# The up projection in products of 256 columns: two feature tiles to a PSUM bank, relu and its square on ScalarE

## The chip, the cores and the metric

The kernel runs on one core of a Trainium2 chip. Its matrix engine is TensorE (PE in the profile, with its weight loads shown apart as PEld), its elementwise engines are VectorE (DVE) and ScalarE (ACT); SyncE (SP) issues most DMAs, and GpSimd (POOL) does little here. Matrix products are written to PSUM, in banks of 2 KB per partition (512 float32 columns); everything else lies in SBUF. The metric is the time of one execution in microseconds of device time. Before the change it is 1237.76 us, the median of three runs (1237.73 to 1237.81).

## What is computed

One layer of a decoder trunk on 256 tokens of width 2048, in float32. A combined input projection feeds a pooling branch and a convolution branch; gated, they are mixed, projected and added to the residual stream. Then comes the part that the change touches, the feed-forward block, with a hidden width of 8192:

```python
h = h + rms_norm(m @ w_o[l], g_post_mix[l])
u = rms_norm(h, g_pre_mlp[l])
f = jnp.square(jax.nn.relu(u @ w_up[l])) @ w_down[l]
h = h + rms_norm(f, g_post_mlp[l])
```

## The kernel before

**Split products.** Every float32 operand `x` of a matrix product is kept as two parts of a faster matrix type: `hi`, the rounded value, and `lo`, what rounding left over. A product is then the sum of three: hi·hi, hi·lo and lo·hi. For the weights ScalarE writes `hi` (L178) and VectorE subtracts to get `lo` (L181), chunk by chunk: a chunk is 512 rows by 512 columns of a weight matrix, 1 MB, loaded by one DMA from SyncE. `fetch()` (L198) opens the chunk two ahead of the one in use, splits it, and then runs the functions that wait in the list `late`. There are three buffers each for the raw chunk, for `hi` and for `lo`.

**The feed-forward block** runs in four passes `i` over the hidden width (loop at L994). Each pass computes 2048 hidden features for all 256 tokens and then adds their share of the down projection. The up projection of a pass is four blocks `h` of 512 features; a block is one call of `project` (L362), which goes through four chunks of 512 input rows. In a block the weights are the stationary operand, so that the result has features on the partitions and the 256 tokens along the columns. A feature tile is 128 features wide, so a block has four of them, `j`, each with a PSUM bank of its own. For each tile and each of the 16 groups of 128 input rows there are two products, issued by `mm2` (L353): one of 512 columns with `hi` of the weights (L344), whose moving operand holds the hi part of the tokens in its first 256 columns and the lo part in the other 256, and one of 256 columns with `lo` of the weights and the hi part of the tokens (L350). So the two halves of the bank must be added at the end. The first block of the first pass, `up00`, is written out apart (from L892) and is not changed.

**Evacuation of a tile** (L841): ScalarE copies the first half of the bank to SBUF (`halves`, L381), VectorE adds the second half (L383), VectorE multiplies the sum with its maximum with zero, which is relu squared (L844), and later, from the list `late`, ScalarE writes the hi part to `f_act` (L388) and VectorE the lo part (L389). `f_act` is the stationary operand of the down projection.

**The down projection** `project_t` (L600) keeps the tokens' hidden features as the stationary operand and streams the weights, 512 columns to a product (`block_t`, L590). Its last block is written out at the end of the kernel; for the second half of the tokens its 512 columns are cut in two halves of 256 (`last_half`, L1007), so that there the same three products are 256 columns wide, with the stationary operands hi, hi and lo in turn.

**Order.** The kernel sets the order of each engine's instructions by hand: they run on each engine as the program issues them, and engines wait for each other by semaphores. `drain` hands out small pieces of other work (in the first pass, the squares of the residual stream, L786) between the products of a chunk; `flush(1)` runs all but the newest of the `late` functions ahead of an evacuation. The pool `psA` has six banks for accumulators.

Of the kernel before, what the change touches and what calls it, by code (L numbers as in the profile page):

```python
# [8 lines left out]
F32 = mybir.dt.float32  # L9
F32R = mybir.dt.float32r  # L10
AF = mybir.ActivationFunctionType
# [3 lines left out]
P = 128  # L15
CK = 4
CW = 512
# [5 lines left out]
def hybrid_block(ctx: ExitStack, tc: tile.TileContext, ins: dict, out: bass.AP):  # L23
    nc = tc.nc
    x = ins["x"][0]
    meta = ins["meta"]
    T, D = x.shape
# [3 lines left out]
    KD = D // P  # L31
# [18 lines left out]
    big = ctx.enter_context(tc.tile_pool(name="big", bufs=1))  # L50
# [6 lines left out]
    def f32(ap):  # L57
        return ap.bitcast(F32)

    def acc_tile(name):  # L60
        return psA.tile([P, CW], F32, tag="acc", name=name)
# [9 lines left out]
    late = []  # L71
# [5 lines left out]
    def flush(n=0):  # L77
        while len(late) > n:
            late.pop(0)()

    def drain(us=None):

        credit["us"] += us or 0.0
        while pending and (us is None or credit["us"] >= pending[0][0]):
            cost, f = pending[0]
            if f is late and late:
                if us is not None:
                    break
                flush()
            pending.pop(0)  # L90
            if callable(f):
                f()
                if us is not None:
                    credit["us"] -= cost
            elif f is None and us is not None:
                break
        credit["us"] = min(credit["us"], pending[0][0]) if pending else 0.0
# [61 lines left out]
    def open_chunk():  # L159
        n = at["n"]  # L160
        at["n"] += 1
        src, (rows, width) = stream[n]
        raw = raws.tile([P, CK * CW], F32, tag="raw", name=f"raw_{n}")
        if n in spare:
            both = big.tile([P, 2, CK * CW], F32R, tag=spare[n], name=f"parts_{n}")
            hi, lo = both[:, 0, :], both[:, 1, :]
        else:
            hi, lo = part_tile("hi", n), part_tile("lo", n)
        raw, hi, lo = (t.rearrange("p (k c) -> p k c", k=rows) for t in (raw, hi, lo))
        pieces = rows if n < FIRST + 1 else 1  # L170
        k = rows // pieces
        loads = 4 if n < FIRST else 1
        for i in range(loads):
            sl = slice(i * rows // loads, (i + 1) * rows // loads)
            nc.sync.dma_start(raw[:, sl, :], src[:, sl, :])

        def high(sl):
            nc.scalar.copy(hi[:, sl, :], raw[:, sl, :])  # L178

        def low(sl):  # L180
            nc.vector.tensor_sub(lo[:, sl, :], raw[:, sl, :], f32(hi[:, sl, :]))  # L181

        def piece(i):
            def f():
                sl = slice(i * k, (i + 1) * k)
                high(sl)
                low(sl)
            return f
        todo = [piece(i) for i in range(pieces)]
        if n in spare:  # L190
            todo = [lambda: high(slice(0, rows)), lambda: low(slice(0, rows))]
        opened.append((hi, lo, todo))

    def split_pieces(c):
        while opened[c][2]:
            opened[c][2].pop(0)()

    def fetch(ahead=2):  # L198

        for c in range(ahead + 1):  # L200
            if c == len(opened) and at["n"] < len(stream):
                open_chunk()
            if c < len(opened):
                split_pieces(c)
        flush()
        return opened.pop(0)[:2]
# [146 lines left out]
    def mm2(acc, hi, lo, act, k, cs, first, last):  # L353


        mm2_high(acc, hi, act, k, cs, first, stop=last)
        mm2_low(acc, lo, act, k, cs, stop=last)

    def acc_tiles(name, n=CW // P):
        return [acc_tile(f"acc_{name}_{j}") for j in range(n)]  # L360

    def project(act, nk, evac, name, mm=mm2, width=CW, shape=HALF, fill=0.0):  # L362

        ck, cw = shape
        accs = [acc[:, :width] for acc in acc_tiles(name, cw // P)]
        for kc in range(nk // ck):
            hi, lo = fetch()
            for j, acc in enumerate(accs):
                for k in range(ck):
                    kk = kc * ck + k  # L370
                    mm(acc, hi, lo, act, (k, kk), slice(j * P, (j + 1) * P), kk == 0, kk == nk - 1)
                if kc == nk // ck - 1:
                    flush(1)
                    evac(j, acc)
                if fill:
                    drain(fill * P / cw)

    def halves(acc, name):

        t = tmp.tile([P, T], F32, tag="v", bufs=5, name=f"half_{name}")  # L380
        nc.scalar.copy(t, acc[:, :T])  # L381
        s = tmp.tile([P, T], F32, tag="v", bufs=5, name=f"sum_{name}")
        nc.vector.tensor_add(s, t, acc[:, T:])  # L383
        return s

    def split(dst, k, src):
        def f():
            nc.scalar.copy(dst[:, k, 0, :], src)  # L388
            nc.vector.tensor_sub(dst[:, k, 1, :], src, f32(dst[:, k, 0, :]))  # L389
        late.append(f)  # L390
# [209 lines left out]
    def project_t(act, nk, evac, name, fill=0.0):  # L600
        accs = acc_tiles(name, NT)
        for kc in range(nk // CK):
            hi, lo = fetch()
            for t, acc in enumerate(accs):
                block_t(acc, hi, lo, act, kc, nk, t)
                if kc == nk // CK - 1:
                    evac(t, acc)
                if fill:
                    drain(fill / NT)
            while after:  # L610
                after.pop(0)()
# [37 lines left out]
    hi, lo = fetch()  # L649
    for g in range(NG):  # L650
        for j in range(GK):
            q = g * GK + j
            acc = acc_tile(f"acc_grp_{q}")[:, :T]
# [158 lines left out]
    u2 = m  # L812
# [23 lines left out]
    f_act = []  # L836
# [4 lines left out]
    def evac_up(j0):  # L841
        def f(j, acc):
            s = halves(acc, f"up_{j0 + j}")
            nc.vector.scalar_tensor_tensor(s, s, 0.0, s, op0=ALU.max, op1=ALU.mult)  # L844
            split(f_act[(j0 + j) // (KD // 2)], (j0 + j) % (KD // 2), s)
        return f

    assert NT == 2 and NB == 4 and CK == 4  # L850
# [85 lines left out]
    hi, lo = fetch()  # L936
# [3 lines left out]
    for j, acc in enumerate(accs):  # L940
        for k in range(CK):
            kk = 3 * CK + k
            mm2(acc, hi, lo, u2, (k, kk), slice(j * P, (j + 1) * P), False, kk == KD - 1)
        flush(1)
        evac_up(0)(j, acc)
    ssq2 = const.tile([P, NT, NB], F32, name="ssq2")


# [18 lines left out]
    def evac_down(i, n):  # L967
        sl = block(n)

        def f(t, acc):  # L970
            if i == 0:
                nc.vector.tensor_copy(F[:, t, sl], acc)
                return
            nc.vector.tensor_add(F[:, t, sl], F[:, t, sl], acc)
            if i == NP - 1:
                square_of(F[:, t, sl], norm3.ssq, t, n, scale=r2[:, t:t + 1])
                times_g(t, sl)
                if n == NB - 2:
                    norm3.start(t)
        return f  # L980
# [12 lines left out]

    for i in range(NP):  # L994
        for h in range(1 if i == 0 else 0, NB):
            project(u2, KD, evac_up(h * CW // P), f"up{i}{h}", shape=(CK, CW), fill=1.0)
        for n in range(NB):
            if i < NP - 1 or n < NB - 1:
                project_t(f_of, KD, evac_down(i, n), f"dn{i}{n}")
# [11 lines left out]
    n = KD // CK - 3  # L1011
    for kc in range(n):
        hi, lo = fetch()
# [12 lines left out]
    for h, cs in enumerate(col_halves):  # L1026
# [3 lines left out]
        s = tmp.tile([P, HALF_CW], F32, tag="v", bufs=5, name=f"last_{h}")  # L1030
# [37 lines left out]
```

## Time and profile before

| | |
|---|---|
| time, median of 3 runs | 1237.76 us |
| the profiled execution's own time | 1238.2 us |
| its span, first to last instruction | 1236.3 us |
| instructions in the profile | 15686 |
| bytes moved by DMA | 237.22 MB |

The profile is one execution. Its page gives each engine's busy time and, for groups of equal instructions, the count, the busy time in all, the mean of one in ns and what ended the idle time before them. A product's entry in a timeline has its start, its duration and its tile of PSUM; products overlap in the pipeline, so what one of them costs is read from the distance between starts and not from its duration. The rows that matter are quoted in the prediction.

### The profile page before, as it was taken

The numbers are of one execution on the slowest core, as the hardware profiler recorded it, in microseconds if no ns is written. First come the engines' busy times: TensorE is split into PE (matmuls) and PEld (weight loads), VectorE is DVE, ScalarE is ACT, GpSimd is POOL, SyncE is SP. The second block draws the span as 40 slices with busy tenths as digits, with TensorE's granted clock in tenths as the row PEclk, the third lists the DMA queues.
The fourth block names the chain that finished last, engine by engine and source line by source line (L and its number), as shares of the span: only waits on it lengthen the run. The fifth ranks groups of instructions, "written<-read, shape, count | busy, mean of one in ns | idle before, by whom it ended". The sixth has DMA issues, their size and how long they took to land.

```text
span 1236.3 us, 15686 instructions
## 1 busy us (share of the span) xinstructions
PE 1224.7 (99%) x6572; PEld 1061.3 (86%) x6572; DVE 807.6 (65%) x938; ACT 541.9 (44%) x571; POOL 6.2 (0%) x18
## 2 busy tenths in 40 slices
PE   9999999999999999999999999999999999999997
PEld 7999988888888888898888888888888888888886
DVE  5799988999676654585654556654475544556555
ACT  6533334444584433555433345433344433435432
POOL 1000000000000000000000000000000000000000
PEclk9999999999999999999999999999999999999999
DMA  8655556556548656646556566556566556566551
GB/s 260 207 181 179 171 171 204 188 188 204 175 165 298 212 205 204 204 142 200 175 200 197 183 199 200 180 199 200 185 194 204 182 193 204 176 201 203 187 187 68
DMA packets 130757, 237.22 MB, mean 192 GB/s; under 512 B 3985, under 2 KB 29905, under 8 KB 130160
## 3 DMA queue, kind: packets, MB, share of 16 engines
q1 hardware_dynamic: 128768, 229.78, 57.4%
q0 software_dynamic: 768, 4.35, 0.9%
q10 hardware_dynamic: 1152, 2.11, 0.5%
q8 instruction: 51, 0.84, 0.3%
q14 instruction: 18, 0.15, 0.0%
HBM read 234.12 MB, written 2.10 MB: 191 GB/s over the span
## 4 chain that ended last, share of the span: by engine, by line
PE 98%; DVE 1%; DMA 0%; ACT 0%; DVEq 0%; issue 0%; ACTq 0%
PE acc_dn L595 26%; PE acc_up L344 19%; PE acc_gate L595 14%; PE acc_up L350 10%; PE acc_o L595 5%; PE acc_v L339 4%; PE acc_z L339 4%; PE acc_g L339 4%; PE acc_co L595 4%; PE acc_po L595 4%; PE acc_f_last L595 2%; PE acc_o_last L595 2%; DMA x_in<-in_x_dram 0%; PE xt L286 0%; PE ht L820 0%; PE mt L715 0%
## 5 line engine op out<-in xcount | busy, mean ns | idle before, releaser
L181 DVE TENSOR_TENSOR lo<-raw,hi 128x2048 fp32r<-128x2048 f32 (+1 forms) x236 | 495.1, 2101 | 354.5 <-ACT hi L178 354.1
L178 ACT CAST hi<-raw 128x2048 fp32r<-128x2048 f32 (+1 forms) x236 | 413.7, 1757 | 559.3 <-PE acc_dn L595 190.6
L344 PE MATMUL acc_up<-m,hi 128*128 128x512 f32 (+1 forms) x1008 | 339.1, 387 | 0.0
L595 PE MATMUL acc_dn<-hi,f_act 128*128 128x512 f32 x960 | 296.3, 389 | 0.0
L350 PE MATMUL acc_up<-m,lo 128*128 128x256 f32 x992 | 272.5, 277 | 0.0
L344 PEld LDWEIGHTS acc_up<-m,hi 128*128 128x128 f32 x1008 | 187.0, 188 | 39.5
L595 PEld LDWEIGHTS acc_dn<-hi,f_act 128*128 128x128 f32 x960 | 180.2, 188 | 37.5
L595 PE MATMUL acc_dn<-lo,f_act 128*128 128x512 f32 x480 | 186.8, 389 | 0.0
L350 PEld LDWEIGHTS acc_up<-m,lo 128*128 128x128 f32 x992 | 185.2, 188 | 0.1
L595 PE MATMUL acc_gate<-hi,u 128*128 128x512 f32 x512 | 158.6, 390 | 0.0
L405 DVE SCALAR_TENSOR_TENSOR c<-a,taps,c 128x256 f32<-128x256 f32 x240 | 115.4, 483 | 6.6
L595 PEld LDWEIGHTS acc_gate<-hi,u 128*128 128x128 f32 x512 | 96.1, 188 | 20.0
L595 PEld LDWEIGHTS acc_dn<-lo,f_act 128*128 128x128 f32 x480 | 90.1, 188 | 18.5
L595 PE MATMUL acc_gate<-lo,u 128*128 128x512 f32 x256 | 99.6, 389 | 0.0
L595 PE MATMUL acc_o<-hi,m 128*128 128x512 f32 x192 | 59.6, 390 | 0.0
L595 PEld LDWEIGHTS acc_gate<-lo,u 128*128 128x128 f32 x256 | 48.1, 188 | 10.0
L339 PE MATMUL acc_v<-u,hi 128*128 128x272 f32 x256 | 50.6, 295 | 0.0
L339 PE MATMUL acc_z<-u,hi 128*128 128x272 f32 x256 | 48.6, 289 | 0.0
L339 PE MATMUL acc_g<-u,hi 128*128 128x272 f32 x256 | 48.1, 288 | 0.0
L595 PEld LDWEIGHTS acc_o<-hi,m 128*128 128x128 f32 x192 | 36.0, 188 | 7.4
L595 PE MATMUL acc_co<-hi,s_act 128*128 128x512 f32 x128 | 40.4, 391 | 0.0
L339 PEld LDWEIGHTS acc_z<-u,hi 128*128 128x128 f32 x256 | 40.4, 188 | 0.0
(222 smaller groups left out, 1060.8 us busy)
## 6 DMA issues: line engine op xcount, KB each, us to landing
raw<-in_w_up_dram SPq DMA_DIRECT2D x64, 1024.0 KB, 5.4
raw<-in_w_down_dram SPq DMA_DIRECT2D x64, 1024.0 KB, 5.1
raw<-in_w_in_dram SPq DMA_DIRECT2D x54, 1024.0 KB, 5.1
raw<-in_w_o_dram SPq DMA_DIRECT2D x16, 1024.0 KB, 5.1
raw<-in_w_pool_out_dram SPq DMA_DIRECT2D x8, 1024.0 KB, 5.1
raw<-in_w_conv_out_dram SPq DMA_DIRECT2D x8, 1024.0 KB, 5.2
raw<-in_w_in_dram SPq DMA_DIRECT2D x8, 256.0 KB, 7.7
h<-in_x_dram POOLq DMA_DIRECT2D x1, 2048.0 KB, 11.0
```

The source lines that it names most:

```text
L178: nc.scalar.copy(hi[:, sl, :], raw[:, sl, :])
L181: nc.vector.tensor_sub(lo[:, sl, :], raw[:, sl, :], f32(hi[:, sl, :]))
L339: nc.tensor.matmul(acc, w[:, k[0], cs], act[:, k[1], a, off:], start=first and n == 0, stop=last and n == 2)
L344: nc.tensor.matmul(acc.rearrange("p (a t) -> p a t", a=2)[:, :, ts], hi[:, k[0], cs], act[:, k[1], :, off + ts.start:off + ts.stop], start ...
L350: nc.tensor.matmul(acc[:, :T], lo[:, k[0], cs], act[:, k[1], 0, off:], start=False, stop=stop, skip_group_check=True)
L405: nc.vector.scalar_tensor_tensor(c, conv["a"][:, q, i:i + T], taps[:, q, i:i + 1], c, op0=ALU.mult, op1=ALU.add)
L595: nc.tensor.matmul(acc, act(kk)[:, a_, ts_], w_[:, k, :], start=kk == 0 and n == 0, stop=kk == nk - 1 and n == 2)
```

## The change

In the up projection of all blocks but `up00`, `pair_up` takes the place of `project`, and `evac_pair` that of `evac_up`. Two feature tiles share one bank, 256 columns each, so a block takes two banks in place of four. For each tile and group of input rows there are three products of 256 columns: `hi` of the weights with the hi part of the tokens, `hi` with the lo part, `lo` with the hi part, all accumulated in the same 256 columns. Nothing is left to be added, and a bank's evacuation is relu and square on ScalarE, 512 columns wide, into a room in SBUF of two places (`up_room`, in the place that `g_mix` has left); later ScalarE writes the hi parts and VectorE the lo parts of both tiles at once.

```diff
+    def pair_up(i, h, fill):
+        banks = acc_tiles(f"up{i}{h}", CW // P // 2)
+        for kc in range(KD // CK):
+            hi, lo = fetch()
+            for b, bank in enumerate(banks):
+                for j in range(2):
+                    acc = bank[:, j * T:(j + 1) * T]
+                    cs = slice((2 * b + j) * P, (2 * b + j + 1) * P)
+                    for k in range(CK):
+                        kk = kc * CK + k
+                        for n, (w, a) in enumerate(((hi, 0), (hi, 1), (lo, 0))):
+                            nc.tensor.matmul(acc, w[:, k, cs], u2[:, kk, a, :],
+                                             start=j == 0 and kk == 0 and n == 0,
+                                             stop=j == 1 and kk == KD - 1 and n == 2,
+                                             skip_group_check=True)
+                if kc == KD // CK - 1:
+                    flush(1)
+                    evac_pair(h * CW // P + 2 * b, bank)
+                drain(fill / 2)
+
+    def evac_pair(j, bank):
+        s = up_room[:, j // 2 % 2, :]
+        nc.scalar.activation(s, bank, AF.Relu)
+        nc.scalar.activation(s, s, AF.Square)
+        dst = f_act[j // (KD // 2)][:, j % (KD // 2):j % (KD // 2) + 2, :, :]
+        s = s.rearrange("p (j t) -> p j t", j=2)
+
+        def f():
+            nc.scalar.copy(dst[:, :, 0, :], s)
+            nc.vector.tensor_sub(dst[:, :, 1, :], s, f32(dst[:, :, 0, :]))
+        late.append(f)
...
+    up_room = big.tile([P, 2, 2 * T], F32, tag="a", name="up_room")
...
     for i in range(NP):
         for h in range(1 if i == 0 else 0, NB):
-            project(u2, KD, evac_up(h * CW // P), f"up{i}{h}", shape=(CK, CW), fill=1.0)
+            pair_up(i, h, 1.0)
```

## The prediction

> **What bounds the kernel now.** I read the page first: which engine is full, and whether the chain that ended last runs through it.
>
> ```profile
> span 1236.3 us, 15686 instructions
> ...
> PE 1224.7 (99%) x6572; PEld 1061.3 (86%) x6572; DVE 807.6 (65%) x938; ACT 541.9 (44%) x571; POOL 6.2 (0%) x18
> ...
> PE 98%; DVE 1%; DMA 0%; ACT 0%; DVEq 0%; issue 0%; ACTq 0%
> ```
>
> TensorE is never without a product, and the chain of waits is 98% TensorE. A busy share of 99% does not yet say that the products run as fast as they can, since their durations overlap. So next come the busy times by stretch, cut at the ends of the up and down stages (columns: stretch, its length, then busy time and count of PE, PEld, DVE, ACT and POOL, granted clock, DMA share and rate).
>
> ```profile
> 545.70:617.50 71.80, 71.80 (x408) 62.43 (x407) 44.73 (x56) 36.72 (x57) 0.00 (x0) 1.00 0.61 195
> 704.60:791.60 87.00, 87.00 (x513) 77.19 (x513) 51.67 (x57) 39.11 (x44) 0.00 (x0) 1.00 0.61 194
> 1052.80:1139.90 87.10, 87.10 (x514) 77.03 (x513) 51.72 (x57) 39.17 (x44) 0.00 (x0) 1.00 0.61 194
> ```
>
> These are the up projections of the first, second and last pass. In each, TensorE is busy for the whole stretch at the full granted clock (1.00), the DMA engines for 61%, and in a whole pass VectorE for 52 of 87 us and ScalarE for 39. The stage lasts as long as its products take to follow one another. A pass has 4 blocks x 4 tiles x 16 groups = 256 pairs of products, so a pair costs 87.0 / 256 = 340 ns in the second and in the last (87.1); I take it for passes two to four. The timeline of TensorE shows the two members.
>
> ```profile
> 752.71 0.39 PE L344 MATMUL acc_up<-m,hi 128*128 128x512 f32 x1
> 752.94 0.28 PE L350 MATMUL acc_up<-m,lo 128*128 128x256 f32 x1
> 753.05 0.39 PE L344 MATMUL acc_up<-m,hi 128*128 128x512 f32 x1
> 753.28 0.28 PE L350 MATMUL acc_up<-m,lo 128*128 128x256 f32 x1
> 753.39 0.39 PE L344 MATMUL acc_up<-m,hi 128*128 128x512 f32 x1
> ```
>
> Starts are 0.23 and 0.11 us apart in turn, 0.68 us for two pairs: 227 ns for 512 columns, 113 ns for 256, both at the same price per column. The first pass is not like that.
>
> ```profile
> 600.04 0.40 PE L344 MATMUL acc_up<-m,hi 128*128 128x512 f32 x1
> ...
> 602.16 0.40 PE L344 MATMUL acc_up<-m,hi 128*128 128x512 f32 x1
> ```
>
> Six pairs in 2.12 us are 353 ns each, with the same shapes at the same clock. That pass is entered from `up00`, whose first three chunks are all 256 wide; the others are entered from the down projection, all 512 wide. So there is a slower way of running, some 13 ns a pair, and I read it as what a stream of 256-wide products leaves behind.
>
> **The change, part by part.**
>
> *The products.* A pair (512 and 256 columns) becomes three products of 256: the same 768 columns, with one more product and one more weight load, since `hi` is loaded twice. There are 192 pairs in the first pass (three blocks of 64) and 3 x 256 = 768 in the others, 960 in all. The question is what three 256-wide products in a row cost. The nearest row is the end of the kernel, where the last block of the down projection runs just this pattern: 256 columns, stationary operands hi, hi, lo.
>
> ```profile
> 1219.03 0.40 PE L595 MATMUL acc_f_last<-hi,f_act 128*128 128x256 f32 x2
> ...
> 1221.91 0.40 PE L595 MATMUL acc_f_last<-hi,f_act 128*128 128x256 f32 x2
> 1222.15 0.28 PE L595 MATMUL acc_f_last<-lo,f_act 128*128 128x256 f32 x1
> 1222.27 0.40 PE L595 MATMUL acc_f_last<-hi,f_act 128*128 128x256 f32 x2
> ...
> 1226.95 0.40 PE L595 MATMUL acc_f_last<-hi,f_act 128*128 128x256 f32 x2
> ```
>
> The columns are start and duration; "x2" is the two hi products. From 1219.03 to 1226.95 lie 22 groups of three: 7.92 / 22 = 360 ns a group, 120 ns a product, though the 512-wide products just before it ran at 227 ns. Two other stretches bound the price. In `up00` all products are 256 wide, on the very operands of this stage; the chain has them 16 at a time.
>
> ```profile
> 533.10 1.92 PE acc_up L350 x16
> ...
> 542.14 1.88 PE acc_up L350 x16
> ```
>
> That is 120.0 and 117.5 ns a product, so 352.5 ns for three at the lower end. And the input projection already issues three products for each tile and row group (`mm3`), 272 columns wide:
>
> ```profile
> 149.73 0.42 PE L339 MATMUL acc_z<-u,hi 128*128 128x272 f32 x2
> ...
> 152.77 0.42 PE L339 MATMUL acc_z<-u,hi 128*128 128x272 f32 x2
> ```
>
> Eight groups in 3.04 us are 380 ns a group; cut in proportion to 256 columns, 358 ns. Uncut, 380 ns is the upper end, since a narrower product should not cost more. I take 360 ns: it is the same width and the same order of weights, it holds for 7.9 us without a break, and it is reached from a fast stretch.
>
> The sum: passes two to four, 768 x (360 - 340) = 15.4 us; first pass, 192 x (360 - 353.3) = 1.3 us; together 16.6 us more on the path. Its ends: at 352.5 ns, 768 x 12.5 - 192 x 0.8 = 9.4 us; at 380 ns, 768 x 40 + 192 x 26.7 = 35.8 us. Below, at 340 ns, nothing in three passes and 192 x 13.3 = 2.6 us gained in the first.
>
> A rule of the Trainium skill speaks for that last end. Its page "TensorE: Matmul & The Clock Gate", section "Back-to-back issue gap", gives an isolated warm product of N columns as N / 2.4 + 2.5 ns: 215.8 for 512 and 109.2 for 256. By it a third product adds one fixed 2.5 ns, an estimate of 960 x 2.5 = 2.4 us and a time near 1240.2 us. The rows differ from it: 227 ns for 512 columns, and for 256 either 113 or 120 ns, depending on the company. The same section warns that in a stream of loads and products both set the spacing, and with that the 120 ns agrees.
>
> *The evacuation.* These are the groups it removes, and the nearest to those it adds.
>
> ```profile
> L388 ACT CAST f_act<-sum_up 128x256 fp32r<-128x256 f32 x64 | 24.4, 406 | 30.9 <-DVE sum_up L844 29.1
> L381 ACT COPY half_up<-acc_up 128x256 f32<-128x256 f32 x64 | 23.5, 368 | 11.1 <-PE acc_up L350 11.1
> L717 ACT CAST m<-mt 128x512 fp32r<-128x512 f32 x8 | 4.3, 589 | 15.9 <-PE mt L715 15.9
> L786 ACT ACTIVATE ng_offset=None)_3_0_4784<-h 128x512 f32<-128x512 f32 x1 | 0.6, 635 | 0.0
> L844 DVE SCALAR_TENSOR_TENSOR sum_up<-sum_up 128x256 f32<-128x256 f32 x64 | 27.2, 425 | 2.2
> L383 DVE TENSOR_TENSOR sum_up<-half_up,acc_up 128x256 f32<-128x256 f32 x64 | 26.5, 415 | 0.0
> L389 DVE TENSOR_TENSOR f_act<-sum_up,f_act 128x256 fp32r<-128x256 f32 x64 | 25.5, 419 | 0.0
> L718 DVE TENSOR_TENSOR m<-mt,m 128x512 fp32r<-128x512 f32 x8 | 5.2, 686 | 9.1 <-ACT m L717 9.1
> ```
>
> The second number after the bar is the mean of one in ns. A block loses 4 x (425 + 415 + 419) = 5.0 us on VectorE and gains 2 x 686 = 1.4. On ScalarE it loses 4 x (406 + 368) = 3.1 us and gains two each of relu and square (635 each, by L786, the square of 512 columns) and of the hi cast (589): 3.7 us. Over 15 blocks that is 55 us off VectorE and 9 us onto ScalarE. I count both at nothing. VectorE's relief is worth nothing, as no product waits for it; ScalarE's 0.6 us a block lies beside 22 us of products, of which it is busy under 10 (39 of 87 us for four blocks). No other table load comes in: the changed program has the same five.
>
> *The order on ScalarE.* Relu of a block's last bank waits for its last product, and the square follows; behind them stands the next chunk's cast (L178), behind that on VectorE its `lo`. Before, one copy of 0.37 us stood there, now 1.27 us. The cast (1.91 us) and the subtraction (2.29 us) then end some 5.5 us after the block's last product. The chunk is wanted two chunks later, after 2 x 16 x 360 ns = 11.5 us in a block or longer still:
>
> ```profile
> L178 ACT CAST hi<-raw 128x2048 fp32r<-128x2048 f32 x212 | 404.8, 1911 | 559.2 <-PE acc_dn L595 190.6 <-PE acc_up L344 137.2 <-PE acc_gate L595 71.6
> L181 DVE TENSOR_TENSOR lo<-raw,hi 128x2048 fp32r<-128x2048 f32 x212 | 485.7, 2291 | 354.2 <-ACT hi L178 353.8
> 617.51 87.06 PE acc_dn L595 x384
> ```
>
> The casts mostly wait for TensorE to free a buffer (137.2 us of idle time ahead of them in the up stages alone), so they run early, not late. The last two hi and lo writes to `f_act` come behind that cast, some 7 us after the last product; the down projection wants them in the last quarter of its first block, 3/4 x 87.06 / 4 = 16.3 us after it. SyncE's loads keep their order, and come due later as the products take longer. PSUM eases: two banks a block instead of four, of six.
>
> So the profiled execution, 1238.2 us (a span of 1236.3 and 1.9 around it), becomes 1254.8; the median lies 0.4 us below it, and I predict 1237.76 + 16.6 = 1254.4 us.
>
> **The rivals.**
> - *Width costs nothing* (other side). The third product runs like the 256-wide one of passes two to four, 113 ns, and the first pass loses its slow way: 1237.76 - 2.6 = 1235.2 us. For it: 227 and 113 ns show no fixed price per product. Against it: each 256 there follows a 512, so the loads have more time; where 256 follows 256 every row shows 117.5 ns or more. It decides if three in a row keep under about 340 ns. The skill's isolated gap, above, is this case with 2.5 ns added.
> - *The lower price of `up00`* (117.5 ns): 1237.76 + 9.4 = 1247.2 us. For it: those are this stage's own operands. Against it: only some of its groups, the others show 120.0.
> - *The input projection's price*, 380 ns a group: 1237.76 + 35.8 = 1273.6 us. For it: it is the longest run of three products with hi loaded twice. Against it: its products are 16 columns wider.
> - *ScalarE becomes the bound*: the 0.9 us more ahead of the cast (1.27 - 0.37) reach TensorE in 15 blocks, 13.5 us on top of the forecast, 1267.9 us. It decides only if the cast comes 6 us later than now; the 11.5 us of lead speak against it.
>
> **How the numbers follow.** Forecast 0.72, `up00`'s price 0.11, the input projection's 0.08, ScalarE as the bound 0.02, width for nothing 0.07. The range 1246 to 1264 holds the first two and prices up to some 367 ns a group (1237.76 + 768 x 27 + 192 x 13.7 = 1261.1), 0.83 in all; it leaves out both far ends. A difference of 0.2%, 2.5 us, is about what a measurement of this kernel can tell from no change. The last rival ends just beyond it; of its 0.07 I give 0.04 to faster and 0.03, for a part of its gain, to the same. The rest, 0.93, is slower.
>
> **What would show it.** In the changed profile: three products of 256 from start to start in 0.36 us in all four passes, alike in the first and the others; an up stage of 256 x 0.36 = 92.2 us where it was 87.1, and down stages of 87.06 as before; TensorE's weight loads busy nearly all of the stage (they were 77 of 87 us); VectorE's up work gone by some 55 us with no change in the chain; ScalarE idle before its casts as now. I am wrong if a group takes near 0.34 us, if it differs between passes, or if idle time of TensorE appears at block ends.

## The result, and the profile after

The changed kernel takes 1247.81 us, the median of four runs (1247.46 to 1248.01), where four runs of the kernel before have a median of 1237.78 (1237.73 to 1238.02). The ratio is 1.0076, with a 95% interval of 1.0061 to 1.0091: slower by 10.0 us. The forecast was 16.6 us slower; the direction and the place are right, the size is not.

The page of the changed kernel, whose profiled execution took 1247.89 us, shows the same picture of a full TensorE: 960 products more, and a chain that is still 98% TensorE.

```profile
span 1246.0 us, 17439 instructions
...
PE 1235.4 (99%) x7532; PEld 1111.1 (89%) x7532; DVE 760.0 (61%) x788; ACT 554.9 (45%) x541; POOL 6.1 (0%) x18
...
PE 98%; DVE 1%; DMA 0%; ACT 0%; DVEq 0%; issue 0%; ACTq 0%
```

The chain of waits of the changed kernel (start, length, engine, tile, line, number of instructions) names its second half stage by stage, since nothing but products lies in it.

```profile
549.23 67.83 PE acc_up L861 x576
617.07 87.07 PE acc_dn L595 x384
704.13 90.45 PE acc_up L861 x768
794.59 87.06 PE acc_dn L595 x384
...
1059.17 90.45 PE acc_up L861 x768
1149.62 65.31 PE acc_dn L595 x288
1214.93 22.42 PE acc_f_last L595 x144
```

An up stage of passes two to four has 768 products, 256 groups of three, in 90.45 us: 353.3 ns a group, where a pair took 340.0. That is 13.3 ns more, 768 times, 10.2 us. In the first pass 192 groups take 67.83 us, again 353.3 ns a group, the same as its pairs before: nothing gained or lost. The down stages stand at 87.06 us as before. So the sum of the stages, 10.2 us, accounts for the 10.0 us of the runs. The timeline of TensorE shows the three members.

```profile
752.02 0.40 PE L861 MATMUL acc_up<-m,hi 128*128 128x256 f32 x2
752.26 0.28 PE L861 MATMUL acc_up<-m,lo 128*128 128x256 f32 x1
752.38 0.40 PE L861 MATMUL acc_up<-m,hi 128*128 128x256 f32 x2
...
753.08 0.40 PE L861 MATMUL acc_up<-m,hi 128*128 128x256 f32 x2
```

Three groups in 1.06 us, 117.8 ns a product. The busy times of the changed kernel by stretch, in the columns of the prediction, follow for the same three passes.

```profile
549.30:617.00 67.70, 67.70 (x577) 67.70 (x576) 33.24 (x28) 37.06 (x47) 0.00 (x0) 1.00 0.61 190
704.20:794.50 90.30, 90.30 (x769) 90.30 (x768) 40.96 (x23) 41.86 (x36) 0.00 (x0) 1.00 0.60 187
1059.20:1149.50 90.30, 90.30 (x769) 90.30 (x768) 40.98 (x23) 41.90 (x36) 0.00 (x0) 1.00 0.60 187
```

The granted clock is full, the DMA engines no busier than before, VectorE has 11 us less to do in a pass and ScalarE 3 us more. The column of weight loads is new: busy for the whole stretch, where it was 77 of 87 us. What the new evacuation costs, and what ScalarE waits for, stands in the groups and in the view of waits (engine, tile and line, what it waited for: us in all, times, longest).

```profile
L880 DVE TENSOR_TENSOR f_act<-up_room,f_act 128x512 fp32r<-128x512 f32 x30 | 19.3, 686 | 0.0
L874 ACT ACTIVATE up_room<-up_room 128x512 f32<-128x512 f32 x30 | 19.0, 633 | 1.0
L873 ACT ACTIVATE up_room<-acc_up 128x512 f32<-128x512 f32 x30 | 18.0, 600 | 39.0 <-PE acc_up L861 39.0
L879 ACT CAST f_act<-up_room 128x512 fp32r<-128x512 f32 x30 | 17.0, 616 | 0.0
```

```profile
ACT hi L178 <- PE acc_up L861: 136.5, 45, 3.8
...
ACT up_room L873 <- PE acc_up L861: 39.0, 30, 1.6
```

ScalarE's casts still wait for TensorE, for 136.5 us in the up stages where it was 137.2: they are as early as before.

### The profile page after: what moved, and what is told of

It reads as the page before. It is cut to its first block, busy times and chain, and to the rows that moved or that the text cites. A ratio compares the mean times of both kernels' runs of the same rounds, so it can differ in the third digit from the quotient of the medians.

```text
span 1246.0 us, 17439 instructions
## 1 busy us (share of the span) xinstructions
PE 1235.4 (99%) x7532; PEld 1111.1 (89%) x7532; DVE 760.0 (61%) x788; ACT 554.9 (45%) x541; POOL 6.1 (0%) x18
## 4 chain that ended last, share of the span: by engine, by line
PE 98%; DVE 1%; DMA 0%; ACT 0%; DVEq 0%; issue 0%; ACTq 0%
PE acc_up L861 27%; PE acc_dn L595 26%; PE acc_gate L595 14%; PE acc_o L595 5%; PE acc_v L339 4%; PE acc_z L339 4%; PE acc_g L339 4%; PE acc_co L595 3%; PE acc_po L595 3%; PE acc_f_last L595 2%; PE acc_o_last L595 2%; PE acc_up L344 1%; PE acc_up L350 1%; DMA x_in<-in_x_dram 0%; PE xt L286 0%; PE ht L820 0%
## 5 line engine op out<-in xcount | busy, mean ns | idle before, releaser
L861 PE MATMUL acc_up<-m,hi 128*128 128x256 f32 x1920 | 339.4, 282 | 0.0
L861 PEld LDWEIGHTS acc_up<-m,hi 128*128 128x128 f32 x1920 | 296.6, 190 | 0.3
L861 PEld LDWEIGHTS acc_up<-m,lo 128*128 128x128 f32 x960 | 180.2, 188 | 0.0
```

The costliest lines, as they stand in the source:

```text
L861: nc.tensor.matmul(acc, w[:, k, cs], u2[:, kk, a, :], start=j == 0 and kk == 0 and n == 0, stop=j == 1 and kk == KD - 1 and n == 2, skip_g ...
```

## The experiments

Two readings of the 360 ns of the prediction were open: that three 256-wide products in a row have one price, and that the price comes from something else that the two stages do not share. And the prediction's slow way of running, which a stream of 256-wide products is said to leave behind, had been read from one stage only. Where the expectations use letters, A is that slow way, which lasts until a run of 512-wide products; B is its rival, that nothing lasts and each form has its own price; C is a price set by where the weights lie in SBUF; D is a price set by the weight load.

For C a detail of the kernel is needed that the change does not touch. The buffers for `hi` and `lo` of a chunk are a little longer than a chunk, and `part_tile` (L152) starts each at one of four places, 64 bytes apart.

```python
LINE = 16
PLACES = {n: (2, 1) for n in standing_chunks}
...
place = PLACES.get(n, (1, 1))[("hi", "lo").index(tag)]
shift = (place - 1 - 3 * KEYS.index(key)) % 4 * LINE
```

Below, a place is given by what it does, as the offsets of `hi` and of `lo` against the tokens' operand in bytes, modulo 256. Place (2, 1), the one of both kernels, is offsets 64 and 0; in the last block of the down projection, from which the 360 ns came, both operands lie at equal offsets. A group's price is the distance between starts, from the first product of a block to the first of the next, divided by its 64 groups.

**The evacuation alone.** Each tile's relu, square and split go back to VectorE and ScalarE at 256 columns; the products stay as changed.

```diff
-        s = up_room[:, j // 2 % 2, :]
-        nc.scalar.activation(s, bank, AF.Relu)
-        nc.scalar.activation(s, s, AF.Square)
+        for i in range(2):
+            acc = bank[:, i * T:(i + 1) * T]
...
+            nc.vector.tensor_scalar_max(r, acc, 0.0)
...
+            nc.vector.tensor_mul(s, r, r)
+            split(f_act[(j + i) // (KD // 2)], (j + i) % (KD // 2), s)
```

> The products of the change as they are, but a bank is evacuated tile by tile on VectorE (maximum with zero, then the square, 256 columns each, the lo and hi parts per tile as before). If the evacuation is covered, as I costed it, the time stays that of the change, 1247.8 us within 0.4, and a group of three products stays at 353.3 ns. If relu and square on ScalarE cost or save something on the path, it moves by more than 1 us, at the block ends, where TensorE would show idle time.

Measured: 1247.5 us, one run, beside 1237.7 before. One up stage of its chain, and the same stretch in busy times:

```profile
703.84 90.45 PE acc_up L861 x768
```

```profile
703.84:794.29 90.45, 90.45 (x770) 90.45 (x769) 51.68 (x57) 34.90 (x30) 0.00 (x0) 1.00 0.60 187
```

VectorE is back at 52 us and ScalarE 7 us lower, and the stage is 90.45 us to the last digit. The evacuation is worth nothing either way; all 10 us are the products.

**Three products in one block alone.** Only the first block of the second pass is changed, all others are pairs.

```diff
-            pair_up(i, h, 1.0)
+            if i == 1 and h == 0:
+                pair_up(i, h, 1.0)
+            else:
+                project(u2, KD, evac_up(h * CW // P), f"up{i}{h}", shape=(CK, CW), fill=1.0)
```

> Three products of 256 columns only in the first block of the second pass; all other blocks keep pairs of 512 and 256. Theory A (the slow way lasts: a stream of 256-wide products puts TensorE into a slower way of running, which pairs of 512 and 256 do not leave, and a stream of 512-wide products does): the remaining three blocks of the second pass also take 353.3 ns a pair, the third and fourth pass 340; 256 x 13.3 ns = 3.4 us more than before, 1241.2 us. Theory B (each group has the price of its own shape, and the first pass is slow for a reason of its own): only 64 groups cost more, 0.9 us, 1238.6 us, and the later blocks of the second pass stay at 340 ns.

Measured: 1240.54 us beside 1237.7, 2.8 us more. The chain has the changed block; the timeline of TensorE has the pairs in the block behind it.

```profile
704.23 22.61 PE acc_up L861 x192
```

```profile
729.83 0.39 PE L344 MATMUL acc_up<-m,hi 128*128 128x512 f32 x1
...
737.18 0.40 PE L344 MATMUL acc_up<-m,hi 128*128 128x512 f32 x1
```

The changed block's 64 groups take 22.61 us, 353.3 ns each, 0.85 us more than pairs. Between the two rows lie 21 pairs, 350.0 ns each where they took 340.0; so it stays in all three blocks that follow, 192 x 10 = 1.9 us. After the down projection the pairs are back; this is the third pass in TensorE's busy time on this tile (stretch, length, busy and count, clock, DMA share and rate):

```profile
881.00:968.00 87.00, 87.00 (x512) 1.00 0.62 194
```

256 pairs in 87.00 us are 340 ns. That bears out A, in this one run: a slower way outlasts what caused it, though with 350 and not with 353 ns.

**A run of 512-wide products in the first pass.** The kernel before, with the second chunk of the first looped block in another order: first all its sixteen `lo` products, then all its sixteen `hi` ones.

```diff
+            if kc == low_first:
+                for k in range(ck):
+                    for j, acc in enumerate(accs):
+                        mm2_low(acc, lo, act, (k, kc * ck + k), slice(j * P, (j + 1) * P))
+                for k in range(ck):
+                    for j, acc in enumerate(accs):
+                        mm2_high(acc, hi, act, (k, kc * ck + k), slice(j * P, (j + 1) * P), False)
+                drain(fill)
+                continue
```

> The kernel before, with one chunk reordered: in the second chunk of the first pass's first looped block, the sixteen 256-wide products come first and the sixteen 512-wide ones after them. Theory A: the run of 512-wide products restores the fast way, and the 160 pairs that follow in the first pass go from 353.3 to 340 ns: 2.1 us less, 1235.6 us. Theory B: the first pass stays at 353.3 ns a pair and the time at 1237.8 us.

Measured: 1237.27 us beside 1237.7. The run itself, and two pairs in the next block:

```profile
556.66 4.13 PE L344 MATMUL acc_up<-m,hi 128*128 128x512 f32 x17
...
589.80 0.39 PE L344 MATMUL acc_up<-m,hi 128*128 128x512 f32 x1
...
594.00 0.39 PE L344 MATMUL acc_up<-m,hi 128*128 128x512 f32 x1
```

The seventeen starts span 4.13 - 0.39 = 3.74 us, so a 512-wide product takes 234 ns, not 227; behind it, 12 pairs in 4.20 us are 350.0 ns. Neither theory had that: the run took the pairs from 353.3 to 350.0 and no further. So sixteen 512-wide products do not bring the fast way back here, while in the kernel before the down projection behind the same pass is at 227 ns within its first ten products. What makes the difference was not isolated.

**The weights at equal offsets.** The changed kernel, with `hi` and `lo` of the up projection where the last down block has its operands (offsets 0 and 0).

```diff
-    PLACES = {n: (2, 1) for n in standing_chunks}
+    PLACES = {n: (1, 1) for n in standing_chunks}
```

> The change with the weights' hi and lo parts shifted so that both start at the same offset within 256 bytes as the tokens (before, hi lay 64 bytes further on). The last block of the down projection has that placement and took 360 ns a group of three. Theory C (the price of three 256-wide products depends on where weights and tokens lie in SBUF): 360 ns a group in all passes, 960 x 6.7 ns = 6.4 us more than the change, 1254.2 us. If the place does not matter, 353.3 ns and 1247.8 us.

Measured: 1254.59 us beside 1237.7. Its chain:

```profile
549.60 69.11 PE acc_up L861 x576
...
705.77 92.15 PE acc_up L861 x768
```

69.11 / 192 and 92.15 / 256 are 360.0 ns a group in every pass. Moving nothing but `hi` of the weights, by 64 bytes (in `up00`'s first and last chunks too), gives the 360 ns of the last down block and, within 0.2 us, the time of the forecast. So C holds, and the row used in the prediction carried its own place with it.

**Half the width.** In the first block of the second pass each product is cut into two of 128 columns, each with its own weight load.

```diff
+                            parts_n = 2 if (i, h) == (1, 0) else 1
+                            for q in range(parts_n):
+                                ts = slice(q * T // parts_n, (q + 1) * T // parts_n)
...
+                                    acc[:, ts], w[:, k, cs], u2[:, kk, a, ts],
```

> The change, but in the first block of the second pass every product is cut into two of 128 columns (six products and six weight loads a group). Theory D (the weight load sets the price of a 256-wide product): a 128-wide product costs about as much as a 256-wide one, 115 to 118 ns, a group some 700 ns, and the block 64 x 350 ns = 22 us more, 1270 us. If the columns set the price, a 128-wide product costs about 60 ns and the group stays near 353 ns. The transposes of the kernel before, 128 columns with a load each, took 109 ns; by them a group is 654 ns and the time 1267 us, and a load of 109 ns lies just under the 113 ns of the columns.

Measured: 1268.28 us beside 1235.52. The chain's stage and two rows of the timeline inside the block:

```profile
704.34 110.72 PE acc_up L864 x960
```

```profile
710.16 0.61 PE L864 MATMUL acc_up<-m,hi 128*128 128x128 f32 x4
...
713.50 0.50 PE L864 MATMUL acc_up<-m,hi 128*128 128x128 f32 x3
```

Five groups of six products in 3.34 us: 111 ns a product, though it has half the columns. Had the columns set the price, the stage would have stayed near 90 us; it grew by 20.3. So a product with its load took 111 ns whatever its columns would need, and the 113.3 ns of a 256-wide product in the pairs lie just above that. That fits D: with 256 columns, loads and columns need nearly the same time. Whether the load itself or some other cost of each product sets the 111 ns, this run doesn't tell apart.

**A map of places.** The changed kernel, with another place in each of its 15 blocks, the change's own (64, 0) among them as a control.

```diff
+    tries = [(hi_, lo_) for hi_ in range(4) for lo_ in range(4) if (hi_, lo_) != (1, 1)]
+    for i, n0 in enumerate(sorted(standing_chunks)[::FFB]):
+        for h in range(1 if i == 0 else 0, NB):
+            place = tries.pop(0)
+            PLACES.update({n0 + h * (KD // CK) + kc: place for kc in range(KD // CK)})
```

> The change, with another place of the weights in each of its 15 blocks: hi and lo are shifted by 0, 64, 128 or 192 bytes against the tokens (within 256 bytes), in all pairings but equal-equal, which was tried. Theory C: each pairing has a price of its own, steady within its block, between 340 and 380 ns a group; hi by 64 and lo by 0 (the change's own) 353.3 ns as control; hi and lo both by 64 the cheapest, near 347 ns, because the fastest block of the input projection (123.4 ns a product against 125.5 to 126.7 in the others) lay so. If only equal offsets cost more, the other fourteen are alike at 353.3 ns.

Measured: 1244.89 us beside 1235.52. The price of a group in ns, with the offsets of `hi` and `lo`, in the order of the blocks, worked out from the starts:

```
first pass     192,192 340.0   192,0   353.3   192,64  340.0
second pass    192,128 347.2   0,192   353.3   0,64    353.4   0,128   357.3
third pass     64,192  340.3   64,0    353.2   64,64   353.3   64,128  354.7
fourth pass    128,192 350.3   128,0   355.0   128,64  353.4   128,128 356.0
```

The timeline of TensorE in the first of these blocks:

```profile
551.75 0.39 PE L868 MATMUL acc_up<-m,hi 128*128 128x256 f32 x2
...
552.77 0.39 PE L868 MATMUL acc_up<-m,hi 128*128 128x256 f32 x2
```

Three groups in 1.02 us: 340 ns, with the same three products, the same three loads, and straight behind `up00`. So the third product and its load need not cost anything, and a stream of 256-wide products need not leave a slow way behind. The expected cheapest place, 64,64, was not it; the three cheap ones are 192,192, 192,64 and 64,192. The control took 353.2 ns, its usual price.

**Pairs by place.** The kernel before with a place for each pass, to see whether the pairs have such prices too.

```diff
+    for n0, place in zip(sorted(standing_chunks)[::FFB], ((1, 1), (2, 2), (1, 2), (3, 3))):
+        PLACES.update({n: place for n in range(n0 + 4 * (place == (1, 1)), n0 + FFB)})
```

> The kernel before, pairs of 512 and 256 throughout, with one place of the weights per pass: first pass hi and lo at the tokens' offset, second pass both 64 bytes on, third hi at it and lo 64 on, fourth both 128 on. If the slow way of the first pass is kept up by the place (the down projection, with its weights at the tokens' offset, leaves it within some ten products), the first pass returns to 340 ns a pair with equal offsets. If the slow way stays whatever the place, the first pass keeps some 350 ns. In the other passes a pair costs 340 ns if a pair entered from 512-wide products is always fast, and up to 353 where its place does not allow it.

Measured: 1245.63 us beside 1235.52. The second pass (offsets 64, 64) in busy times of TensorE on this tile, and two starts in the third (0, 64):

```profile
704.10:794.50 90.40, 90.38 (x512) 1.00 0.59 186
```

```profile
884.88 0.39 PE L347 MATMUL acc_up<-m,hi 128*128 128x512 f32 x1
...
894.93 0.39 PE L347 MATMUL acc_up<-m,hi 128*128 128x512 f32 x1
```

Pairs take 353.3 ns in the first pass (0, 0), 90.40 / 256 = 353 in the second, 10.05 / 29 = 347 in the third and, from starts, 351 in the fourth (128, 128). Equal offsets didn't free the first pass. Of the places tried, each in one pass, pairs cost 340 only at the one that the kernel before has, and there in passes two to four alone; the change kept that place, which is a good one for pairs and not for threes.

**All at 192, 192: threes, pairs, and the input projection.** Three kernels take the map's first block to the whole up projection: the changed kernel, the kernel before, and the changed kernel with the input projection's chunks moved as well (to 192, 192 against its own tokens' operand).

```diff
-    PLACES = {n: (2, 1) for n in standing_chunks}
+    PLACES = {n: (0, 0) for n in standing_chunks}
```

```diff
-    PLACES.update({n: (n // FIRST % 4, n // FIRST // 4) for n in range(first_products)})
+    PLACES.update({n: (3, 3) for n in range(first_products)})
```

> The change with hi and lo of the weights 192 bytes on from the tokens (within 256 bytes) in all blocks, the pairing that gave 340.0 ns a group in the map. If that price was a matter of place alone, all fifteen blocks take 340 ns, the first pass too, and the time is 13.3 x 960 = 12.8 us under the change, 1235.0 us. If it depended on the neighbouring blocks or on that pass, some blocks go back to 353 ns.

> The kernel before with that same placement, pairs of 512 and 256. If the place sets the price for either form, 340 ns a pair in all four passes, 1235.2 us, the same as the change there: the form of the products then costs nothing by itself. If pairs and threes want different places, more than that.

> The change with the placement of 192 bytes, and the input projection's weights moved so as well (its three products of 272 columns took 123.4 to 126.7 ns each). If the place sets the price there too, 272 columns fall to 272/256 x 113.3 = 120.4 ns, 12 blocks x 96 products x some 5.4 ns = 6.2 us less: near 1229 us, faster than either kernel. If 272-wide products are slow for another reason, no change there and 1235 us.

Measured, beside 1237.89 us (seven runs): the changed kernel 1247.87 us, ratio 1.0083 (1.0066 to 1.0100); the kernel before 1244.12, ratio 1.0053 (1.0038 to 1.0068); with the input projection 1248.72, ratio 1.0091 (1.0076 to 1.0106). A stage of the first one's chain, and one of the third one's input projection:

```profile
704.15 90.45 PE acc_up L861 x768
```

```profile
115.42 48.64 PE acc_z L339 x384
```

The threes are at 353.3 ns in all 15 blocks, not at the map's 340.0: the same place has two prices, so the place isn't all of it. What came before differs, `up00` among it, which was moved here too. The pairs of the second one have yet another price, in its timeline:

```profile
729.73 0.39 PE L344 MATMUL acc_up<-m,hi 128*128 128x512 f32 x1
...
739.84 0.39 PE L344 MATMUL acc_up<-m,hi 128*128 128x512 f32 x1
```

29 pairs in 10.11 us are 349 ns, the same in all 15 blocks. The input projection gained nothing: 48.64 us for 384 products is 126.7 ns each, and in the kernel before it was 48.58. Its other eight blocks, at 123.4 to 126.6 ns a product in the kernel before, rose to 126.5 to 126.7, and the kernel takes 0.85 us more than the first of the three.

**Two places.** The changed kernel with `up00` left as it was, the rest of the first pass at 192, 192 and the later passes at 64, 192.

```diff
-    PLACES = {n: (2, 1) for n in standing_chunks}
+    FFB = NB * KD // CK
+    PLACES = {n: (2, 0) for n in standing_chunks}
+    first_pass = sorted(standing_chunks)[:FFB]
+    PLACES.update({n: (2, 1) for n in first_pass[:KD // CK]})
+    PLACES.update({n: (0, 0) for n in first_pass[KD // CK:]})
```

> The change with the two placements that ran at 340 ns in the map, each entered as it was there: in the first pass, after the unchanged first block, hi and lo 192 bytes on from the tokens; in passes two to four, entered from the down projection, hi 64 and lo 192 on. Theory E (TensorE falls into one of a few steady ways of running; which one is fixed by the placement together with the products it comes from, and it then lasts): 340 ns a group in all fifteen blocks, 960 x 13.3 ns = 12.8 us under the change, near 1235 us, some 2.5 us under the kernel before, whose first pass is slow. If the map's 340 ns came from changing the place at each block, the later blocks of a pass go back to 353 ns.

Measured: 1237.50 us, the median of ten runs (1234.66 to 1237.98), beside 1237.71, the median of thirteen (1234.83 to 1238.05); the ratio is 0.9994 (0.9984 to 1.0004). Its chain:

```profile
549.30 67.84 PE acc_up L865 x576
...
704.24 87.06 PE acc_up L865 x768
```

All of the change's loss is gone. 87.06 us are 340.0 ns a group in passes two to four, as for the pairs, and the first pass of this execution is at 353.3. The ten runs fall in two clusters, four at 1234.7 to 1235.7 and six at 1237.4 to 1238.0; the kernel before has three of its thirteen at 1234.8 to 1235.5, too, and its one run of 1235.52 beside three experiments above is another. The gap is 192 x 13.3 ns = 2.6 us, the first pass: it fits that this pass goes one way or the other from execution to execution, though only the upper cluster was profiled.

This also changes the reading of the map. The first block of that pass has here the same products at the same addresses, with the same ones before them, that gave 340.0 ns there (on another chip), and it took 353.4. So not even place and history together fix the price. The traces show the same in `up00`: its first sixteen products, the same instructions at the same addresses and on the same chip, follow each other at 118 ns from the second one on in the profile of the run with three products in one block, and at 113 ns from the fifth one on in that of the evacuation alone.

**One place.** As the last, with 64, 192 in the first pass too.

```diff
-    PLACES.update({n: (0, 0) for n in first_pass[KD // CK:]})
```

> As the run before, but the placement that held 340 ns in passes two to four (hi 64 and lo 192 bytes on from the tokens) in the looped blocks of the first pass too; only the first block, written out apart, keeps its old place. If that placement sets the fast way whatever comes before, the first pass takes 340 ns a group in every execution, and the time is near 1235 us without executions at 1237.7. If the entry from the first block decides there, the first pass stays at 353 ns in most executions and the time is 1237.5 us again.

Measured: 1235.13 us, the median of eleven runs (1234.90 to 1235.39), beside 1237.74, the median of fifteen (1236.86 to 1238.33); the ratio is 0.998 (0.9971 to 0.9989). That is 0.2% under the kernel before and 1.0% under the changed kernel. Its chain:

```profile
549.47 65.33 PE acc_up L864 x576
...
701.86 87.06 PE acc_up L864 x768
```

340 ns a group in all four passes. Against the changed kernel only the addresses of the looped blocks' `lo` parts differ, by one place (offset 192 in place of 0), and 12.7 us go: 1247.81 - 1235.13 (the kernel before took 1237.78 us beside the one and 1237.74 beside the other). The 2.6 us under the kernel before are what its slow first pass costs, 192 x 13.3 ns; its own faster executions above, 1234.8 to 1235.5 us, are as short. Pairs were not run at 64, 192, so it isn't shown that three products in place of a pair gain anything by themselves.

## Why the prediction was right, and where it was wrong

**The bound** was right: TensorE's own pace is the time. The stages add up to 10.2 us of the 10.0, and in the up stages TensorE is busy from end to end.

**The price of three** is the step that failed: "I take 360 ns: it is the same width and the same order of weights". It measured 353.3 ns, so that the term 768 x 20 is 768 x 13.3, and 192 x 6.7 is nothing; together 6.4 us too much. The form was right and so was the count. What that row didn't share with the up projection was the place of its operands: put the weights there, and the price is 360.0 and the time 1254.59 us. The range held the measured time by 1.8 us, because its low end had room for the rival made of `up00`'s price.

**The rival of `up00`**, 352.5 ns and 1247.2 us, came out nearly exact, but by luck. The row with 117.5 ns a product (542.14) streams against `lo` of `up00`'s third chunk, which lies in a buffer of its own (`parts` in the trace) and not at the looped blocks' offsets. The chunk that has those offsets is the first: the row with 120.0 ns (533.10) is its `lo`, at 0, and the row of the same chain just ahead of that is its `hi`, at 64.

```profile
531.25 1.84 PE acc_up L344 x16
```

That is 115.0 ns a product, 113 from the seventh one on, all of them 256 wide. So the sentence "where 256 follows 256 every row shows 117.5 ns or more" misread the profile: a row of the kernel before spoke for the rival that width costs nothing. Two smaller misreadings move no number: `up00`'s last chunk is pairs, so not all its products are 256 wide, and an "x2" in the last down block is not one group's two hi products but the end of one group and the start of the next.

**The slow way** that a stream of 256-wide products leaves behind was half right. Pairs do inherit it from threes (350 ns behind the changed block). But pairs entered from the down projection run at 347 to 353 ns at other places, and threes behind `up00` at 340 at theirs. The prediction had one cause where there are at least three: place, what came before, and a share that differs from execution to execution.

**The rival "width costs nothing"** was held at 0.07 with 1235.2 us. At the place given it is false; at offsets 64, 192 it is what happens, 1235.13 us. So neither the count of products nor that of loads is the price as such. That goes for the sentence with 2.5 ns for a third product as well: it cost 13.3 ns at the change's place and 0.0 at the other.

**The evacuation at nothing** was right, and put back it changes no stage by 0.1 us. Its durations were right to some 40 ns (600, 633, 616 and 686 ns against 635, 635, 589 and 686), which by the groups' sums is 19.0 + 18.0 + 17.0 us in and 60/64 of 24.4 + 23.5 us out, 9.1 us more on ScalarE, as forecast. The engines' busy times moved otherwise: VectorE's fell by 47.6 us, not 55, though the groups' own sums do fall by 55 (60/64 of 79.2 out, 19.3 in), and ScalarE's rose by 13.0. Instructions that follow each other closely overlap in the trace by some 0.1 us (below, the one at 732.08 starts before that at 729.87 has taken its 2.29 us), and the busy time counts the overlap once; with fewer instructions there is less of it.

**The order on ScalarE** was right. The timeline of ScalarE and VectorE after the first block of the second pass, whose last product ends at 726.7 us, shows it.

```profile
726.78 0.60 ACT L873 ACTIVATE up_room<-acc_up 128x512 f32<-128x512 f32 x1 [1.56 <-PE acc_up L861]
727.41 0.63 ACT L874 ACTIVATE up_room<-up_room 128x512 f32<-128x512 f32 x1
727.95 1.89 ACT L178 CAST hi<-raw 128x2048 fp32r<-128x2048 f32 x1
729.74 1.14 ACT L879 CAST f_act<-up_room 128x512 fp32r<-128x512 f32 x2
```

```profile
729.87 2.29 DVE L181 TENSOR_TENSOR lo<-raw,hi 128x2048 fp32r<-128x2048 f32 x1 [4.63 <-ACT hi L178]
732.08 1.29 DVE L880 TENSOR_TENSOR f_act<-up_room,f_act 128x512 fp32r<-128x512 f32 x2
```

The chunk's `lo` is done at 732.2, 5.4 us after that product (5.5 forecast), and the last write to `f_act` at 733.4, 6.6 us after it (7). TensorE is busy for all of the stage, so no product waits for either, and the rival of a bound on ScalarE had nothing to stand on.

**The signs** named: alike in all four passes, yes, though at 0.353 and not 0.36 us, and the stage at 90.45 and not 92.2; weight loads busy all of the stage, yes. That last sign misleads as an explanation. In the fastest kernel, with 340 ns a group, the loads are as busy, as its window shows:

```profile
701.86:788.92 87.06, 87.06 (x769) 87.06 (x769) 40.98 (x23) 41.94 (x36) 0.00 (x0) 1.00 0.63 194
```

**What stays open** is the mechanism. Shown is that the price follows the weights' address within 256 bytes and what ran before, and that with both the same it can still differ from one execution to the next. That the nearly equal needs of loads and columns make the pace settle in one of several steady rhythms is argued from the 111 ns and the 113.3 ns only, and not shown. The tokens' operand was never moved, so whether the offset against it counts or the weights' own address isn't told apart; nor is what resets the pace in the down projection.

## What to carry to other kernels

A price read off another stage carries that stage's operand addresses and its history with it, not only its shape; before a form is judged, measure it at several offsets of its operands, over whole blocks, from start to start, and in several executions. A change of form should bring a new choice of addresses: the place at which pairs took 340 ns cost threes 353.3, and threes have their own at 340. An engine that is busy all the time at its full clock can still have time to give: here the up stage went from 90.45 to 87.06 us by moving one operand by 64 bytes. Whether a stage of 512-wide products alone depends on addresses as much was not tried.

## What the hardware showed that was not expected

- The same three products with the same loads ran at 340, 353 or 360 ns a group, as one part of the weights was shifted by 64 bytes; a pair of 512 and 256 columns ran at 340, 347, 349, 350, 351 or 353 ns. Each price held for whole blocks.
- A part of the weights at the tokens' own offset never went with the cheapest price of threes: in the map, the changed kernel and the run with equal offsets, every block with `hi` or `lo` at offset 0 took 353 ns a group or more. Alone, sixteen 256-wide products in a row with `up00`'s first `lo` took 120.0 ns each in all eleven profiles that have it at offset 0, and 117.8 or 113.3 ns in the three that have it at 192.
- The Trainium skill says in "TensorE: Matmul & The Clock Gate", section "Step-by-step: what each phase is for", that loading the next weights takes no SBUF read bandwidth from the running product. No run here shows why the address of the weights counts, but a pace that follows it by 6% isn't what that rule leads one to expect.
- A product of 128 columns took 111 ns, nearly as long as one of 256 (113.3). The same page of the Trainium skill gives a load of P columns, in its section "LDWEIGHTS (loading the stationary operand)", as P / 1.2 ns, which is an estimate of 106.7 ns for 128. That lies 4% below the measured pace and so fits a price set by the load, without showing it.
- One program at one place gave two times, 1234.8 to 1235.5 and 1237.2 to 1238.1 us for the kernel before in one set of thirteen runs, 2.6 us apart by their means; at offsets 64, 192 eleven runs of the threes kept within 0.5 us.
